# Second block of a two-block fp32 kernel: the order of a head pair's projections, a pair's end cut in two steps, and separate buffers

## The chip, the cores and the metric

One core of one Trainium2 chip runs the whole program. The metric is the device time of one execution in microseconds, the median over the runs shown.

## The reference

The program computes two blocks of two layers each over 512 tokens of width 1024, in fp32. The change touches the token mixing of the second block's layers, which has three kinds of heads of width 64:

```python
def layer(x, ...):                       # second block, cut
    a = dilated_mixture(q, k, v, bias_tab)            # 6 heads
    b = diff_attention(q1, q2, k1, k2, v, lam, bias_tab)   # 4 heads, then rms_norm per head
    c = causal_attention(q, k, v)                     # 6 heads, k and v from a 128-wide latent
...
def diff_attention(q1, q2, k1, k2, v, lam, bias_tab):
    a = probs(q1, k1) - lam * probs(q2, k2)           # two softmaxes per head
    return jnp.einsum('bhqk,bkhd->bqhd', a.astype(v.dtype), v)
```

Behind the mixing lie an output projection, a norm and a gated feed-forward network with 1024-wide weights.

## The kernel before

Every large product is computed three times: an operand is split into a high and a low part (`split`, lines 165 and 169), and `mm3` (lines 212, 213, 214) issues high by high, low by high and high by low. A matmul covers 128 rows of contraction by 512 tokens. TensorE also does all transposes (against `ident`), so ScalarE (ACT) and VectorE (DVE) spend their time on copies out of PSUM, splits of freshly loaded weights (`wh`, `wl`) and the softmax.

`second_mix` treats the heads in pairs, in the order of the list `UNITS`: differential 0, latent 0, differential 1, latent 1, dilated 0, latent 2, dilated 1, dilated 2. A pair has these parts.

- **Projection.** For a dilated or differential pair Q, K and V are each 24 matmuls `acc<-xt,wh` (`proj_t`), all into one of three PSUM buffers `acc`. A latent pair has 18 matmuls `acc<-ct,wh` in all, since its inputs are narrow.
- **V** (`vpair`, lines 991 to 1005): ACT copies the projection from PSUM to `vt` (line 996), TensorE transposes it in four pieces (line 999) into another `acc`, ACT takes the high part and DVE the low part (lines 1003, 1004).
- **Q and K of a differential pair** are split in four pieces of 32 rows, each an ACT instruction and behind it a DVE one on the same rows; GpSimd (POOL) makes a copy of each.
- **Attention** (`att2`): per head four score tiles of rising width (line 1025), a DVE instruction that adds the bias table and takes the maximum (line 1028), ACT's exp (line 1032), transposes of the weights (line 1058), a split, and the product with V (lines 1072 to 1075) whose two halves ACT and DVE put into `heads` (lines 1084, 1085). A differential head has two such softmaxes, combined on DVE (line 1048).
- **The pair's end** (`fin`): a factor per token and head, `inv`, is laid out along the rows by a DVE copy (line 1113, into `iv` or `sq`), transposed by TensorE (line 1118) and multiplied into the heads (lines 1120, 1122). A differential pair first takes the sum of squares (ACT line 1176, TensorE `half2` line 1179, DVE lines 1183 and 1184, POOL lines 219 and 222, DVE line 1186).

The order on each engine comes from a list scheduler that goes by priorities. The loop at the end of `second_mix` (lines 1306 to 1318) emits the projection of the next pair and then, at a priority raised by `AHEAD` (102), the two heads of this pair and the end of the pair before it:

```python
            if i + 1 < len(UNITS):
                nxt = proj(i + 1)
            with self.tc.high_priority(offset=AHEAD):
                for finish in att():
                    finish()
                if fin is not None:
                    fin()
            fin = fn
```

So the projection matmuls of the next pair fill TensorE while softmax runs on the other engines. During a turn whose next pair is a latent one there are 18 matmuls of 512 columns to fill with, otherwise 72; during the last turn there are none. `vt`, `iv`, `sq` and the latent pair's `qu` share one ring of two SBUF buffers (tag "vt").

Of the kernel before, what the change touches and what calls it, by code (L numbers as in the profile page):

```python
# [16 lines left out]
P = 128  # L17
# [100 lines left out]
class _Kernel:  # L118
# [107 lines left out]
    def setup(self):  # L226
# [20 lines left out]
        self.cF = self.small(4 * KT + P, "cF", 1)  # L247
# [707 lines left out]
    def second(self):  # L955
        tc, nc, A = self.tc, self.nc, self.A
        with ExitStack() as es:
# [4 lines left out]
            self.ropek = self.sp.tile([P, NX, 64], F32, name="ropek")  # L962
            nc.gpsimd.dma_start(self.ropek, A["ropek"])
# [125 lines left out]
    def second_mix(self, l, pool):  # L1089
# [8 lines left out]
        dl = pool.tile([P, 4, 32], F32, tag="dl", bufs=1, name="dl")  # L1098
        src = A["diff_lambda_2"][l]
        nc.gpsimd.dma_start(dl, bass.AP(tensor=src.tensor, offset=src.offset, ap=[[0, P], [32, 4], [1, 32]]))  # L1100
        pr = pool.tile([P, 2, 32], F32, tag="dlp", bufs=1, name="dlp")
        nc.vector.tensor_tensor(pr, dl[:, 0:4:2, :], dl[:, 1:4:2, :], op=ALU.mult)
        e2 = self.small(2, "lam2", 2)
        nc.vector.reduce_sum(e2, pr, axis=mybir.AxisListType.X)
        nc.scalar.activation(e2, e2, AF.Exp)
        nlam = self.small(1, "lam", 2)
        nc.vector.scalar_tensor_tensor(nlam, e2[:, 1:2], -li, e2[:, 0:1], op0=ALU.add, op1=ALU.subtract)
# [3 lines left out]
        def by_row(o, r8, sg, sq):  # L1111

            nc.vector.tensor_copy(
                sq.rearrange("p (a b) -> p a b", b=64), r8.unsqueeze(2).to_broadcast([P, 8, 64])
            )
            tp = self.tps()
            for t in range(NX):
                nc.tensor.transpose(tp[:, t * P : (t + 1) * P], sq[:, t * P : (t + 1) * P], self.ident)
# [4 lines left out]

        def dilated(p, o):
            Q, K, L = self.qk(pool), self.qk(pool), self.qk(pool)
            ps = self.proj_t(W, p * P)
# [9 lines left out]
            V = self.vpair(pool, self.proj_t(W, 768 + p * P))  # L1136
# [7 lines left out]
            def fin():  # L1144
                by_row(o, inv, None, pool.tile([P, SEQ], F32, tag="vt", bufs=2, name="iv"))

            return att, fin

        def differential(p, o):

            b0 = 1152 + p * P
# [39 lines left out]
        def latent(p, o):  # L1191
# [6 lines left out]
            for j in range(2):  # L1198
                kh, kl = Kb[j]
                self.split(kh[0:64], kl[0:64], pk[j * 64 : j * 64 + 64])  # L1200
# [307 lines left out]
```

## Time and profile before

| What | Value |
|---|---|
| median of 3 runs | 1983.33 us (1978.05 to 1986.85) |
| the profiled execution | 1981.64 us, its span 1979.9 us |
| mean granted TensorE clock | 0.993 of full speed |
| TensorE busy | 1901.3 us, 96% |
| TensorE weight loads (beside matmuls) | 1560.8 us, 79% |
| VectorE busy | 1203.6 us, 61% |
| ScalarE busy | 894.1 us, 45% |
| GpSimd busy | 169.7 us, 9% |

The span is the profiled execution of the program from its first to its last recorded instruction; the 1.7 us between it and the execution's own time lie around it. The mixing of the second block's two layers runs from about 731 to 914 us and from about 1370 to 1553 us. A row of the timeline is a start, a length, an engine, a line and the tiles; what stands in brackets is how long the engine had been idle and what released it. In a row of matmuls the lengths overlap, so the pace is read from start to start.

### The profile page before, as it was taken

How to read it: one execution, taken by the hardware profiler on the slowest of the kernel's cores; microseconds unless marked ns; L12 is line 12 of the kernel's file. 1: busy time of each engine (PE TensorE's matmuls, PEld its weight loads, DVE VectorE, ACT ScalarE, POOL GpSimd, SP SyncE). 2: the span in 40 equal slices, each digit the busy share in tenths (PEclk: the TensorE clock that was granted, in tenths of full speed). 3: DMA queues.
4: the chain of work that ended last, by engine and by line, in shares of the span. 5: the costliest groups of instructions: out<-in, count | busy, mean ns of one | idle time of the engine just before them, and what ended most of it. 6: DMA issues, size and time to landing. Idle time of an engine off the chain costs nothing.

```text
span 1979.9 us, 25710 instructions
## 1 busy us (share of the span) xinstructions
PE 1901.3 (96%) x9564; PEld 1560.8 (79%) x9564; DVE 1203.6 (61%) x2350; ACT 894.1 (45%) x1744; POOL 169.7 (9%) x299
## 2 busy tenths in 40 slices
PE   6999999999999999899999999999999999999997
PEld 3878788778878777777888888887777788888886
DVE  3759984375988578776733434366876664243444
ACT  4736662384755558665221322215866432132220
POOL 2100000030000132101200000012211010000001
PEclk9999999999999999999999999999999999999999
DMA  8414342042332361223432324325122332232421
GB/s 291 148 54 140 96 128 85 23 160 79 118 87 63 111 167 43 65 86 111 119 96 85 107 75 117 94 80 130 41 64 95 124 107 96 75 117 64 128 75 43
DMA packets 220448, 197.19 MB, mean 100 GB/s; under 512 B 30154, under 2 KB 178128, under 8 KB 220324
## 3 DMA queue, kind: packets, MB, share of 16 engines
q1 hardware_dynamic: 209940, 160.32, 27.3%
q0 software_dynamic: 10384, 35.24, 5.2%
q8 instruction: 75, 1.23, 0.3%
q14 instruction: 49, 0.40, 0.1%
HBM read 187.09 MB, written 12.03 MB: 101 GB/s over the span
## 4 chain that ended last, share of the span: by engine, by line
PE 80%; ACT 6%; DVE 5%; issue 2%; DMA 1%; POOL 1%; POOLq 0%; DVEq 0%; ACTq 0%; SPq 0%
PE acc L212 22%; PE acc L213 22%; PE acc L214 22%; PE sps L1025 2%; PE tps L792 1%; PE tps L1058 1%; ACT wh L165 1%; PE pv L803 1%; PE pv L1074 1%; PE pv L804 1%; DVE wl L169 1%; PE pv L1075 1%; PE tps L410 1%; DMA wr<-in_w_mod_dram 1%; ACT L L1032 1%
## 5 line engine op out<-in xcount | busy, mean ns | idle before, releaser
L165 ACT ACTIVATE wh<-wr 128x1024 fp32r<-128x1024 f32 (+3 forms) x299 | 311.9, 1045 | 605.3 <-PE acc L213 262.5
L169 DVE TENSOR_TENSOR wl<-wr,wh 128x1024 fp32r<-128x1024 f32 (+3 forms) x299 | 358.3, 1202 | 259.2 <-ACT wh L165 256.5
L212 PE MATMUL acc<-xt,wh 128*128 128x512 f32 (+1 forms) x1200 | 465.9, 388 | 2.1 <-DVE kb L169 1.7
L214 PE MATMUL acc<-xt,wl 128*128 128x512 f32 (+1 forms) x1200 | 464.7, 387 | 0.0
L213 PE MATMUL acc<-xt,wh 128*128 128x512 f32 (+1 forms) x1200 | 463.7, 386 | 0.0
L212 PEld LDWEIGHTS acc<-xt,wh 128*128 128x128 f32 x1200 | 226.2, 188 | 41.5 <-DVE kb L169 2.4
L214 PEld LDWEIGHTS acc<-xt,wl 128*128 128x128 f32 x1200 | 226.1, 188 | 39.8
L213 PEld LDWEIGHTS acc<-xt,wh 128*128 128x128 f32 x1200 | 226.2, 188 | 39.2
L212 PE MATMUL acc<-wh,ht 128*128 128x512 f32 (+1 forms) x494 | 193.1, 391 | 1.3 <-ACT ht L165 1.1
L213 PE MATMUL acc<-wl,ht 128*128 128x512 f32 (+1 forms) x494 | 192.1, 389 | 0.0
L214 PE MATMUL acc<-wh,ht 128*128 128x512 f32 (+1 forms) x494 | 191.7, 388 | 0.0
L165 ACT ACTIVATE pth<-tps 128x384 fp32r<-128x384 f32 (+1 forms) x176 | 90.1, 536 | 90.4 <-PE tps L792 48.4
L169 DVE TENSOR_TENSOR ptl<-tps,pth 128x384 fp32r<-128x384 f32 (+1 forms) x176 | 104.7, 614 | 25.4 <-ACT pth L165 24.1
L212 PEld LDWEIGHTS acc<-wh,ht 128*128 128x128 f32 x494 | 92.9, 188 | 23.0 <-ACT ht L165 2.6
L214 PEld LDWEIGHTS acc<-wh,ht 128*128 128x128 f32 x494 | 93.0, 188 | 21.2 <-DVE ht L169 0.4
L213 PEld LDWEIGHTS acc<-wl,ht 128*128 128x128 f32 x494 | 92.9, 188 | 20.0
L1032 ACT ACTIVATE L<-L,nm 128x512 f32<-128x512 f32 (+3 forms) x160 | 89.0, 557 | 31.2 <-DVE nm L1028 29.8
L1429 DVE SCALAR_TENSOR_TENSOR h<-h,acc 128x512 f32<-128x512 f32 (+1 forms) x50 | 33.2, 665 | 114.9 <-PE acc L214 114.9
L1395 DVE SCALAR_TENSOR_TENSOR th<-th,acc 128x512 f32<-128x512 f32 x42 | 28.9, 688 | 113.3 <-PE acc L214 113.1
L1028 DVE CUSTOM_DVE_ANT_0 L<-sps,T 128x512 f32<-128x512 f32 (+3 forms) x160 | 75.4, 487 | 25.4 <-PE sps L1025 23.5
L219 POOL TENSOR_SCALAR rv<-bna 128x1 f32<-128x1 f32 x16 | 18.8, 1173 | 789.0 <-DVE bna L1324 789.0
L214 PE MATMUL acc<-wh,xt 128*128 128x256 f32 (+2 forms) x256 | 85.1, 333 | 1.0 <-DVE xt L169 0.8
(317 smaller groups left out, 3352.2 us busy)
## 6 DMA issues: line engine op xcount, KB each, us to landing
wr<-in_w_in_dram SPq DMA_DIRECT2D x66, 512.0 KB, 4.6
wr<-in_w_gate_dram SPq DMA_DIRECT2D x44, 512.0 KB, 3.8
wr<-in_w_up_dram SPq DMA_DIRECT2D x44, 512.0 KB, 3.9
wr<-in_w_down_dram SPq DMA_DIRECT2D x42, 512.0 KB, 3.5
wr<-in_w_mod_dram SPq DMA_DIRECT2D x40, 512.0 KB, 4.5
wr<-in_w_o_dram SPq DMA_DIRECT2D x32, 256.0 KB, 3.6
T<-skew POOLq DMA_DIRECT2D x26, 256.0 KB, 2.9
x<-in_x_dram POOLq DMA_DIRECT2D x8, 512.0 KB, 7.1
```

Of the source, the lines that this page charges most:

```text
L165: self.nc.scalar.activation(out, in_, AF.Copy, scale=scale)
L169: self.nc.vector.tensor_tensor(out, in_, hi.bitcast(F32), op=ALU.subtract)
L212: mm(ps, lh, rh, start=(first and i == 0), stop=False)
L213: mm(ps, lh, rl, start=False, stop=False)
L214: mm(ps, ll, rh, start=False, stop=(last and i == n - 1))
L410: nc.tensor.transpose(v[:, k, :], src[:, (kb * 4 + k) * P : (kb * 4 + k + 1) * P], self.ident)
L792: nc.tensor.transpose(tp[:, hq * P : (hq + 1) * P], Ps[hq][:, i * P : (i + 1) * P], self.ident)
L1025: nc.tensor.matmul(ps[:, :w], x[:, tok], y[:, :w], start=(k == 0), stop=(k == len(s) - 1))
L1028: nc.vector.tensor_tensor_reduce(lc, ps[:, :n], T[:, SEQ - n : SEQ], 1.0, 3.0e38, op0=ALU.add, op1=ALU.min, accum_out=nm[:, i : i + 1],)
L1032: nc.scalar.activation(lc, lc, AF.Exp, bias=nm[:, i : i + 1], scale=-1.0, accum_out=sums[:, i : i + 1])
L1395: nc.vector.scalar_tensor_tensor(th, th, 0.5, pu, op0=ALU.mult, op1=ALU.mult)
L1429: nc.vector.scalar_tensor_tensor(h[:, c], h[:, c], ALPHA if gi == 0 else 1.0, ps, op0=ALU.mult, op1=ALU.add)
```

## The change

In `second_mix`, for all three kinds, V is projected first and copied to `vt` at once (`vcopy`); Q and K are projected behind it, and the transposes and the split of V come last. A pair's end becomes a list of two steps: laying out the factors (with the sum of squares ahead of it for a differential pair), and the transposes with the multiplication. One step is emitted behind each of the two heads of the next pair, where before the whole end came behind both. The laid-out factors have a buffer of their own (tag "iv", one buffer). Two small loads move: `ropek` is loaded per layer in place of once, and the differential pair's `lam` is computed inside the same short-lived pool as the latent inputs; `cF` of the conditioning goes to another pool.

```diff
+    def vcopy(self, pool, ps):
+        vt = pool.tile([P, SEQ], F32, tag="vt", bufs=2, name="vt")
+        self.nc.scalar.copy(vt, ps)
+        return vt
+
-    def vpair(self, pool, ps):
+    def vpair(self, pool, vt):
 
         nc = self.nc
-        vt = pool.tile([P, SEQ], F32, tag="vt", bufs=2, name="vt")
-        nc.scalar.copy(vt, ps)
...
-        def by_row(o, r8, sg, sq):
-
+        def spread(r8, iv=None):
+            iv = iv or pool.tile([P, SEQ], F32, tag="iv", bufs=1, name="iv")
             nc.vector.tensor_copy(
-                sq.rearrange("p (a b) -> p a b", b=64), r8.unsqueeze(2).to_broadcast([P, 8, 64])
+                iv.rearrange("p (a b) -> p a b", b=64), r8.unsqueeze(2).to_broadcast([P, 8, 64])
             )
+            return iv
+
+        def by_row(o, iv, sg=None):
+
             tp = self.tps()
...
+        def two_steps(o, inv):
+            ivs = []
+            return [lambda: ivs.append(spread(inv)), lambda: by_row(o, ivs[0])]
+
         def dilated(p, o):
             Q, K, L = self.qk(pool), self.qk(pool), self.qk(pool)
+            vt = self.vcopy(pool, self.proj_t(W, 768 + p * P))
             ps = self.proj_t(W, p * P)
...
-            V = self.vpair(pool, self.proj_t(W, 768 + p * P))
+            V = self.vpair(pool, vt)
...
         def differential(p, o):
 
             b0 = 1152 + p * P
+            vt = self.vcopy(pool, self.proj_t(W, b0 + 512))
...
-            V = self.vpair(pool, self.proj_t(W, b0 + 512))
+            V = self.vpair(pool, vt)
...
-            def fin():
-                sq = pool.tile([P, SEQ], F32, tag="vt", bufs=2, name="sq")
+            r8s = []
+
+            def sums():
+                sq = pool.tile([P, SEQ], F32, tag="iv", bufs=1, name="sq")
...
-                by_row(o, r8, sg, sq)
-
-            return att, fin
+                r8s.append(spread(r8, sq))
+
+            return att, [sums, lambda: by_row(o, r8s[0], sg)]
...
+            cp = es.enter_context(self.tc.tile_pool(name="c0", bufs=1, reuse_waits="tile"))
+            ropek = cp.tile([P, NX, 64], F32, tag="ropek", name="ropek")
+            nc.gpsimd.dma_start(ropek, A["ropek"])
+            nlam = lam(cp)
...
-        fin = None
+        fins = []
         for i in range(len(UNITS)):
             att, fn = nxt
             if i + 1 < len(UNITS):
@@ -1311,10 +1327,11 @@
             with self.tc.high_priority(offset=AHEAD):
                 for finish in att():
                     finish()
-                if fin is not None:
-                    fin()
-            fin = fn
-        fin()
+                    if fins:
+                        fins.pop(0)()
+            fins = fn
+        for f in fins:
+            f()
```

The number of matmuls stays at 9564. How the order moves is shown at three places on TensorE. In the changed kernel the lines of `second_mix` and `att2` are counted on by one or more (scores 1026, transposes of weights 1059, of V 1000, of factors 1127, sum of squares 1193).

**The second differential pair's turn, its first head.** Before, the score tiles `sps<-qk` stand between the 24 matmuls of the pair's own V projection, the end of which is:

```order
L1025 MATMUL sps_8046<-qk_7758,qk_7710 128x384
L214 MATMUL acc_7781<-xt_105,wl_7778 128x512
L1025 MATMUL sps_8047<-qk_7759,qk_7711 128x384
L212 MATMUL acc_7781<-xt_105,wh_7777 128x512
L213 MATMUL acc_7781<-xt_106,wh_7777 128x512
L1025 MATMUL sps_8054<-qk_7758,qk_7710 128x512
L214 MATMUL acc_7781<-xt_105,wl_7778 128x512
L1025 MATMUL sps_8055<-qk_7759,qk_7711 128x512
```

Here `acc_7781` collects V, and `qk_7710` and `qk_7711` are the pieces of the first head's K. In the changed kernel the last projection matmul of the pair (`acc_7766`, now K) stands ahead of the transposes of V and of every score of the pair; what is left to fill with are the latent pair's `acc<-ct`:

```order
L214 MATMUL acc_7766<-xt_105,wl_7763 128x512
L1059 MATMUL tps_7939<-ident_84,L_7901 128x128 x2
L1000 MATMUL acc_7808<-ident_84,vt_7710 128x128
L1059 MATMUL tps_7930<-ident_84,L_7901 128x128
L1059 MATMUL tps_7939<-ident_84,L_7901 128x128
L1000 MATMUL acc_7808<-ident_84,vt_7710 128x128 x3
L212 MATMUL acc_7973<-ct_7057,wh_7453 128x512
L213 MATMUL acc_7973<-ct_7058,wh_7453 128x512
L1075 MATMUL pv_7929<-pth_7935,V_7479 128x512
L1026 MATMUL sps_8030<-qk_7791,qk_7743 128x256
```

The scores moved from among the pair's own projection to behind it.

**The end of the second differential pair, as the first dilated pair starts.** Before, the sum of squares (`half2`) and the transposes of the factors (`ident,sq`) stand close together:

```order
L214 MATMUL acc_8478<-ct_7068,wl_7454 128x512
L1179 MATMUL tps_8458<-half2_7043,sq_8456 128x2 x4
L999 MATMUL acc_8484<-ident_84,vt_8482 128x128 x4
L212 MATMUL acc_8492<-ct_7068,wh_7453 128x512
L213 MATMUL acc_8492<-ct_7069,wh_7453 128x512
L1118 MATMUL tps_8472<-ident_84,sq_8456 128x128
L1058 MATMUL tps_8554<-ident_84,L_8529 128x128 x4
```

Between the two stand the transposes of one V and two matmuls of 512 columns. In the changed kernel the sum of squares stands half a turn earlier, among the dilated pair's projection matmuls:

```order
L213 MATMUL acc_8245<-xt_106,wh_8241 128x512
L214 MATMUL acc_8245<-xt_105,wl_8242 128x512
L212 MATMUL acc_8245<-xt_105,wh_8241 128x512
L1193 MATMUL tps_8392<-half2_7041,sq_8390 128x2
L213 MATMUL acc_8245<-xt_106,wh_8241 128x512
```

The transposes of its factors (`tps_8472`) follow 73 rows further down, past the dilated pair's last projection matmul and its first scores.

**The last turn, the third dilated pair.** Before, the transposes of the first head's weights `L` and of V stand right behind the last projection matmul:

```order
L214 MATMUL acc<-xt,wl 128x512
L1118 MATMUL tps<-ident,iv 128x128
L1058 MATMUL tps<-ident,L 128x128 x4
L1118 MATMUL tps<-ident,iv 128x128 x3
L999 MATMUL acc<-ident,vt 128x128 x4
L1058 MATMUL tps<-ident,L 128x128 x5
L1074 MATMUL pv<-pth,V 128x512
```

All 16 score matmuls of the pair stand further up, among the projection matmuls. In the changed kernel they stand behind the last of these, the first 8 of them ahead of any transpose of weights:

```order
L214 MATMUL acc<-xt,wl 128x512
L1127 MATMUL tps<-ident,iv 128x128 x4
L1000 MATMUL acc<-ident,vt 128x128 x4
L1026 MATMUL sps<-qk 128x256 x4
L1026 MATMUL sps<-qk 128x384 x2
L1026 MATMUL sps<-qk 128x512 x2
L1059 MATMUL tps<-ident,L 128x128 x3
```

The scores lost the projection matmuls that stood between them.

## Rows read from the trace of the kernel before

**Rows 1.** The page: busy time of the engines, and the chain that ended last.

```profile
PE 1901.3 (96%) x9564; PEld 1560.8 (79%) x9564; DVE 1203.6 (61%) x2350; ACT 894.1 (45%) x1744; POOL 169.7 (9%) x299
PE 80%; ACT 6%; DVE 5%; issue 2%; DMA 1%; POOL 1%; POOLq 0%; DVEq 0%; ACTq 0%; SPq 0%
```

**Rows 2.** Windows: stretch, length, busy time by engine, granted clock, DMA share, GB/s.

```profile
960.00:1300.00 340.00, 339.51 (x1579) 281.88 (x1578) 137.19 (x158) 89.12 (x110) 3.95 (x5) 1.00 0.33 100
731.00:746.00 15.00, 10.79 (x54) 7.33 (x52) 12.08 (x30) 12.48 (x28) 3.26 (x5) 1.00 0.25 72
770.00:796.00 26.00, 22.65 (x121) 17.11 (x120) 22.43 (x66) 21.53 (x60) 6.11 (x10) 1.00 0.15 41
819.00:846.00 27.00, 23.12 (x124) 18.65 (x124) 18.39 (x46) 19.01 (x44) 5.28 (x8) 0.94 0.24 69
902.00:914.00 12.00, 8.71 (x53) 6.21 (x52) 8.12 (x15) 7.11 (x15) 0.00 (x0) 1.00 0.20 66
sum 183.00, PE 166.60 PEld 130.44 DVE 142.63 ACT 129.61 POOL 27.40; mean PE 23.80 PEld 18.64 DVE 20.38 ACT 18.52 POOL 3.91
sum 183.00, PE 167.98 PEld 131.31 DVE 141.10 ACT 127.67 POOL 26.37; mean PE 24.00 PEld 18.76 DVE 20.16 ACT 18.24 POOL 3.77
```

**Rows 3.** Waits of TensorE, whole run: total us, times, longest.

```profile
PE acc L999 <- ACT vt L996: 8.3, 10, 1.4
PE tps L1118 <- DVE sq L1113: 4.8, 2, 2.4
```

**Rows 4.** Timeline of TensorE, 777 to 796 us, first layer.

```profile
777.42 0.40 PE L213 MATMUL acc<-xt,wh 128*128 128x512 f32 x1
777.65 0.39 PE L214 MATMUL acc<-xt,wl 128*128 128x512 f32 x1
...
795.97 0.50 PE L212 MATMUL acc<-xt,wh 128*128 128x512 f32 x1 [0.49 <-DVE kb L169]
```

**Rows 5.** Timeline of DVE, 776 to 784 us.

```profile
776.82 0.70 DVE L169 TENSOR_TENSOR qk<-acc,qk 32x512 fp32r<-32x512 f32 x1
...
778.17 0.69 DVE L1028 CUSTOM_DVE_ANT_0 L<-sps,T 128x512 f32<-128x512 f32 x1
...
778.78 0.69 DVE L169 TENSOR_TENSOR ptl<-tps,pth 128x512 fp32r<-128x512 f32 x1
...
781.57 1.93 DVE L1048 SCALAR_TENSOR_TENSOR L<-L,sum 128x128 f32<-128x128 f32 x4
```

**Rows 6.** Timeline of ACT and DVE, 729 to 731 us: pieces of a differential K.

```profile
729.00 0.59 ACT L165 ACTIVATE qk<-acc 32x512 fp32r<-32x512 f32 x1 [1.50 <-DVE qk L169]
730.34 0.59 ACT L165 ACTIVATE qk<-acc 32x512 fp32r<-32x512 f32 x1 [0.75 <-DVE qk L169]
```

**Rows 7.** Timeline of TensorE, 830 to 836 us, first layer.

```profile
830.27 0.66 PE L999 MATMUL acc<-ident,vt 128*128 128x128 f32 x4 [1.40 <-ACT vt L996]
830.68 0.48 PE L212 MATMUL acc<-ct,wh 128*128 128x512 f32 x1
...
835.99 0.33 PE L1118 MATMUL tps<-ident,sq 128*128 128x128 f32 x1 [2.40 <-DVE sq L1113]
```

**Rows 8.** POOL in the same stretch.

```profile
833.41 1.67 POOL L222 TENSOR_TENSOR rr<-rv,mhalf 128x8 f32<-128x8 f32 x1
```

**Rows 9.** Windows of 4 us: columns as in rows 2.

```profile
832.00:836.00 4.00, 1.60 (x12) 1.16 (x12) 1.79 (x6) 1.95 (x3) 2.68 (x4) 1.00 0.39 131
836.00:840.00 4.00, 4.00 (x17) 3.32 (x18) 2.47 (x4) 1.29 (x3) 0.40 (x1) 0.62 0.02 4
786.00:790.00 4.00, 2.40 (x10) 1.60 (x9) 2.54 (x11) 2.09 (x7) 1.86 (x2) 1.00 0.00 0
```

**Rows 10.** Timeline of TensorE and DVE, 905 to 914 us: the last turn.

```profile
905.48 1.00 PE L1058 MATMUL tps<-ident,L 128*128 128x128 f32 x5 [1.28 <-DVE ptl L169]
...
914.07 0.50 PE L212 MATMUL acc<-wh,ht 128*128 128x512 f32 x1 [0.56 <-ACT ht L165]
```

**Rows 11.** POOL ahead of the mixing, first layer.

```profile
703.88 0.25 POOL L1253 MEMSET xs<- 128x64 f32 x2 [4.02 <-DMA xs<-x]
```

More of the change, by code (lines that the diff above doesn't have):

```diff
@@ L246, in setup @@
         nc.vector.scalar_tensor_tensor(th, th, 1.0, c16, op0=ALU.add, op1=ALU.mult)
-        self.cF = self.small(4 * KT + P, "cF", 1)
+        self.cF = vp.tile([P, 4 * KT + P], F32, tag="cF", name="cF")
         nc.gpsimd.memset(self.cF, 0.0)
@@ L961, in second @@
             nc.gpsimd.dma_start(self.rope2, A["rope2"])
-            self.ropek = self.sp.tile([P, NX, 64], F32, name="ropek")
-            nc.gpsimd.dma_start(self.ropek, A["ropek"])
             self.half2 = self.sp.tile([P, 2], F32, name="half2")
@@ L1097, in second_mix, with lam @@
         li = 0.8 - 0.6 * math.exp(-0.3 * l)
[L1098 to L1107, printed above, removed]
+        def lam(pool):
+            dl = pool.tile([P, 4, 32], F32, tag="dl", bufs=1, name="dl")
+            src = A["diff_lambda_2"][l]
+            nc.gpsimd.dma_start(dl, bass.AP(tensor=src.tensor, offset=src.offset, ap=[[0, P], [32, 4], [1, 32]]))
+            pr = pool.tile([P, 2, 32], F32, tag="dlp", bufs=1, name="dlp")
+            nc.vector.tensor_tensor(pr, dl[:, 0:4:2, :], dl[:, 1:4:2, :], op=ALU.mult)
+            e2 = self.small(2, "lam2", 2)
+            nc.vector.reduce_sum(e2, pr, axis=mybir.AxisListType.X)
+            nc.scalar.activation(e2, e2, AF.Exp)
+            nlam = self.small(1, "lam", 2)
+            nc.vector.scalar_tensor_tensor(nlam, e2[:, 1:2], -li, e2[:, 0:1], op0=ALU.add, op1=ALU.subtract)
+            return nlam
         sg = self.small(1, "sg", 2)
         nc.vector.tensor_scalar(sg, self.col[:, 102 + l : 103 + l], 1.0 - li, None, ALU.mult)
-        def by_row(o, r8, sg, sq):
+        def spread(r8, iv=None):
+            iv = iv or pool.tile([P, SEQ], F32, tag="iv", bufs=1, name="iv")
             nc.vector.tensor_copy(
-                sq.rearrange("p (a b) -> p a b", b=64), r8.unsqueeze(2).to_broadcast([P, 8, 64])
+                iv.rearrange("p (a b) -> p a b", b=64), r8.unsqueeze(2).to_broadcast([P, 8, 64])
             )
+            return iv
+        def by_row(o, iv, sg=None):
             tp = self.tps()
             for t in range(NX):
-                nc.tensor.transpose(tp[:, t * P : (t + 1) * P], sq[:, t * P : (t + 1) * P], self.ident)
+                nc.tensor.transpose(tp[:, t * P : (t + 1) * P], iv[:, t * P : (t + 1) * P], self.ident)
             if sg is None:
@@ L1194, in latent @@
             self.mm3(pk, [(ukh[:, 1, hc], ukl[:, 1, hc], cT[2][0], cT[2][1])])
-            V = self.vpair(pool, pk)
+            vt = self.vcopy(pool, pk)
             pk = self.acc()
@@ L1200, in latent @@
                 self.split(kh[0:64], kl[0:64], pk[j * 64 : j * 64 + 64])
+            V = self.vpair(pool, vt)
             qs = []
@@ L1220, in att @@
                     yield self.att2(t2, [[(qh, kh), (qh, kl), (ql, kh)]], Tc, V, j, o, inv[:, j:8:2])
[L1222 to L1225 removed]
+            return att, two_steps(o, inv)
         def proj(i):
@@ L1240, in second_mix @@
         ws = self.wset(W, KT, 2, 1920, 416)
-        with self.tc.tile_pool(name="c0", bufs=1, reuse_waits="tile") as cp:
+        with ExitStack() as es:
+            cp = es.enter_context(self.tc.tile_pool(name="c0", bufs=1, reuse_waits="tile"))
+            ropek = cp.tile([P, NX, 64], F32, tag="ropek", name="ropek")
+            nc.gpsimd.dma_start(ropek, A["ropek"])
+            nlam = lam(cp)
             xss = []
@@ L1256, in second_mix @@
                 t1 = cp.tile([P, 2, 32], F32, tag="kt", bufs=2, name="kt")
-                rk = self.ropek[:, t, :]
+                rk = ropek[:, t, :]
                 nc.vector.tensor_tensor(t1[:, 0, :], ps[:, 384:416], rk[:, 0:32], op=ALU.mult)
```

7 lines of the change are left out of this document (1 added, 6 removed).

## The prediction

> **What bounds the kernel now.** I read the page's busy times first. TensorE is busy 96% of the span and makes 80% of the chain that ended last; DVE has 61%, ACT 45% [rows 1]. So a microsecond counts where TensorE stands still, and only there. The windows tell where that is [rows 2]. From 960 to 1300 us, in the feed-forward part, it idles 0.5 of 340 us. In the mixing it is busy 166.6 of 183 us in the first layer and 168.0 in the second: 16.4 and 15.0 us idle, 31.4 in all, 1.6% of the run. That is the most that the change can win by filling gaps, beside what the clock gives back. It adds no matmul; each unit of fill that it puts into one gap is taken from another.
>
> The list of waits names two gaps that the change aims at. TensorE's V transposes waited for ACT's copy `vt` ten times, 8.3 us in all; the transposes of the factors of a differential pair waited for DVE's `sq` twice, 2.4 us each [rows 3]. The timeline shows the second one: the first factor transpose starts at 835.99 after 2.40 us of waiting [rows 7], while POOL takes 1.67 us for eight columns of the reciprocal root [rows 8] with short DVE steps on both sides. [...]
>
> **The change part by part.** The sum is made against the profiled execution, 1981.64 us (span 1979.9 and 1.7 around it), which is 1.7 under the median of the runs. 0.5%, about what a measurement of this kernel can tell from no change, is 9.9 us.
>
> *V first, its transposes last.* The copy `vt` then has 48 matmuls of cover; at 0.23 us from start to start [rows 4] that is 11 us, so the wait L999 <- L996 goes. But what the V projection used to cover loses its cover. In the old order a pair's scores start while its own V is projected; now K comes last, and no score can start before K is projected and split. With three long projections ahead of it the pair loses up to 24 x 0.23 = 5.5 us of fill. Where the pair after it has 72 matmuls to give, that costs nothing, since they follow at once; this holds for pairs with a dilated or differential one behind them. It hurts where a pair's scores stand ahead of a latent pair's 18 matmuls: the first differential pair at the start (d), the second one (a), the first dilated pair (b); and in the last turn, which has none (c).
>
> (a) *Second differential pair* (770 to 796 us; before, TensorE idle 26.00 - 22.65 = 3.4 us with DVE busy 22.4 of 26 [rows 2]). By the new order, DVE's work from the first low piece of K to the instruction that frees an `acc` for new fill is: four pieces of K at 0.70; two heads' weight splits, 0.69 for 512 columns and less for the narrower two, 1.6 per head; four softmaxes of four tiles, of which the widest takes 0.69, some 1.64 to 1.96 each; the combination 1.93; two V, two `kb`, one `qu`, two `heads`, a factor copy and a multiplication of 512 columns, 0.4 to 0.7 each, 5.6 together; 1 us of small ones [rows 5]. That is 20 to 22.7 us. TensorE has in the same stretch 18 matmuls at 0.23 (4.1), 16 score tiles (2.6, scaled by columns), the products with V of two heads (2.3), and 25 transposes, four of which take 0.41 from start to start [rows 7]: 2.5; with the refill after small pieces, 12 to 13.5. Idle is then 6.5 to 10.7, that is 3.1 to 7.3 more. I take +5, the middle.
>
> The K pieces bear on this. In the trace ACT's next piece waits for DVE's last, 1.34 us from one to the next, though each lies in other rows [rows 6]; four in series are 5.4 us. [...]
>
> (b) *First dilated pair* (819 to 846 us; idle 27.00 - 23.12 = 3.9 [rows 2], with the clock 5.4). Here both waits lay: V's 1.40 and the factors' 2.40 [rows 7]. The *two-step end* takes the sum of squares half a turn forward, among projection matmuls, so the POOL step of 1.67 has that long and the 2.40 goes. By the same count DVE has 14.8 to 15.4 us in the new stretch and TensorE 12 to 13.5: idle 1.3 to 3.4. Gain between 2.0 and 4.1; I take -3.
>
> (c) *The last turn* (902 to 914 us; 8.7 busy, idle 3.3, of which 1.28 wait for a weight split and 0.56 for the last `ht` [rows 2, 10]). The 16 score tiles, 2.6 us of TensorE, now fall here, with a softmax chain ahead of the first transpose. If the chain lengthens by just these, idle stays: 0. If all the fill that stood among them (16 matmuls, 3.7 us) turns into waiting, +3.7. V no longer gates the first product, which speaks for the low end; I take +0.5.
>
> (d) *Start of the mixing* (731 to 746 us, idle 4.2 [rows 2]). Its V waits go, but DVE, busy 12.1 of the 15 us, brings the first scores no earlier, because K's pieces now come after the last projection matmul. 0, between -2 (the waits won) and +1.
>
> (e) *The laid-out factors' own buffer* takes a DVE or ACT instruction's wait for `vt` away; those copies are 0.4 us and covered by fill: 0. *`ropek` and `lam`* put two POOL DMAs per layer ahead of the reciprocal root of the latent inputs. In the first layer POOL waited there for a transfer of `xs` until 703.88 anyway [rows 11]; 0, to +1 if the load is late. `cF`: the memory only, 0.
>
> (f) *The clock.* The stall of (b) is gone; but the stretch of (a) is some 60% busy. The window with 2.40 of 4 us busy did not lower the clock afterwards, that with 1.60 did [rows 9]. +0.5, between 0 and +3.
>
> Per layer: 5 - 3 + 0.5 + 0 + 0 + 0.5 = +3; two layers +6: 1981.6 + 6 = **1988 us** (rounded).
>
> **The rivals.** *Faster:* the waits come back whole. V's 8.3 and the factors' 4.8 [rows 3] with two times 1.5 of clock are 16; if (a) and (c) are hidden because the scheduler's order lets the latent fill last, 1981.6 - 16 = 1966 us. For it: that these waits end nowhere else in the list. Against: DVE's 22.4 of 26 us in (a), which needs the 24 matmuls beside it.
>
> *Slower:* DVE becomes the bound of (a), with the clock falling there. Idle at its upper end is +7.3, a clock fall like that of 836 us 1.5, the tail 2.5, with the gain in (b) 2: +9.3 per layer, 2000 us. It decides once more than about 5.5 us of idle is added in (a). For it: nothing but 18 matmuls stands between the last K matmul and the next projection. [...]
>
> *The change does not do what it says:* the steps are only emitted earlier, and the scheduler's order leaves the same waits in sum, moved: 0, 1982 us. The order shows the factor transposes apart from their sum of squares, so this is unlikely as a whole; it falls within no change.
>
> **How the numbers follow.** The forecast and the case of no effect, whose ends lie within 9.9 us of the profiled run: 0.49. Faster 0.22, slower 0.29, as (a) has more known cost than the waits have certain gain. The range goes to both rivals' times less a bit on the fast side and more on the slow one, where the terms (c) and (f) can add: 1969 to 2006. Left out are a tenth on each side.
>
> **What would show it.** Right: no row for V transposes waiting on `vt`, none of 2.4 us for `sq`; TensorE busy in the window of the second differential pair falls by 4 to 6 us against the length, and the releaser of its gaps is DVE (`kb`, `V` or `nm`); the granted clock stays 1.00 around the first dilated pair; the matmul count is 9564. Wrong: (a) idles no more than 4 us, or the last turn is over 3 us longer in idle, or a new wait on POOL ahead of the mixing.

## The result and the profile after

The changed kernel takes 2010.14 us (median of four runs, 2004.67 to 2010.71) against 1983.51: the ratio is 1.0129, interval 1.0112 to 1.0147. It is slower by 26.6 us; 1988 was forecast, with 2006 as the upper end.

The page of the changed kernel, span and busy times, against [rows 1]:

```profile
span 2008.7 us, 25702 instructions
PE 1918.3 (96%) x9564; PEld 1570.4 (78%) x9564; DVE 1206.0 (60%) x2350; ACT 893.1 (44%) x1744; POOL 167.9 (8%) x300
```

The work is the same: as many matmuls, DVE and ACT instructions, and DVE and ACT within 3 us of their busy times. TensorE is busy 17 us longer on the same matmuls, which is the first sign of the clock (its mean granted clock is 0.986, against 0.993 before), and idle some 12 us longer. The list of its waits, to be read against [rows 3]:

```profile
PE sps L1026 <- DVE nm L1029: 13.5, 22, 2.3
PE sps L1026 <- DVE qk L169: 8.1, 6, 2.4
...
PE tps L1127 <- DVE iv L1118: 4.1, 2, 2.1
PE acc L1000 <- DVE V L1005: 3.5, 2, 1.8
PE sps L1026 <- POOL qk L1149: 2.9, 6, 0.6
```

The two waits that the change aimed at are gone: V's transposes no longer wait for `vt`, nor the factors of the differential pairs for 2.4 us. In their place the scores wait, for K's split (`qk`, 8.1 us) and for the softmax that frees their PSUM buffer (`nm`, 13.5).

For the rest of this text each layer's mixing is cut at the same five places of TensorE's order in every kernel: the first transpose of the latent inputs, the first dilated or differential projection matmul behind each of the three latent pairs' 18 matmuls, and the first output projection matmul. I call the four stretches start, second differential, first dilated and rest; the middle two hold the turn ahead of that pair and its own scores. The windows of these stretches, first layer; the sum is over both layers' eight. Kernel before:

```profile
731.35:746.27 14.92, 10.44 (x52) 7.11 (x50) 12.00 (x32) 12.72 (x30) 3.01 (x5) 1.00 0.25 72
746.27:795.97 49.70, 46.23 (x246) 35.94 (x246) 44.78 (x127) 40.49 (x107) 10.44 (x16) 1.00 0.16 43
795.97:846.48 50.51, 45.90 (x245) 36.87 (x246) 37.98 (x90) 33.81 (x78) 7.50 (x12) 0.97 0.23 63
846.48:914.07 67.59, 63.68 (x339) 50.32 (x337) 47.59 (x108) 42.63 (x102) 6.11 (x10) 1.00 0.28 90
...
sum 367.87, PE 335.27 PEld 262.33 DVE 284.85 ACT 259.42 POOL 54.07; mean PE 41.91 PEld 32.79 DVE 35.61 ACT 32.43 POOL 6.76
```

Changed kernel:

```profile
732.63:752.93 20.30, 14.64 (x53) 9.96 (x51) 16.58 (x42) 15.35 (x37) 5.63 (x9) 0.78 0.22 66
752.93:810.95 58.02, 50.34 (x245) 38.34 (x244) 45.65 (x123) 40.30 (x104) 10.08 (x16) 0.91 0.12 32
810.95:857.40 46.45, 44.23 (x235) 34.65 (x234) 33.50 (x82) 30.68 (x72) 6.93 (x10) 0.99 0.24 69
857.40:929.20 71.80, 66.02 (x348) 52.03 (x346) 50.95 (x113) 44.97 (x106) 9.16 (x16) 0.99 0.33 109
...
sum 392.64, PE 349.39 PEld 269.34 DVE 293.33 ACT 262.62 POOL 63.59; mean PE 43.67 PEld 33.67 DVE 36.67 ACT 32.83 POOL 7.95
```

Start +5.4, second differential +8.3, first dilated -4.1, rest +4.2; in the second layer +3.7, +8.0, -4.4, +3.6. Of the 28.8 us that the span grew, 24.8 lie here, 1.3 ahead of the first mixing, 2.0 between the two and 0.7 behind. The 24.8 split by these windows: idle (length less TensorE's busy time) goes from 32.6 to 43.3, +10.7. What the lower clock cost, each stretch's busy time times one less its granted clock, goes from 5.3 to 15.8 over the eight, +10.5; this is an estimate. The other 3.6 stays unexplained.

The cut ahead of the rest moved a little: ten matmuls that stood in the first dilated stretch before (TensorE's 245 against 235) now stand in the rest (339 against 348). At the 0.11 to 0.23 us from start to start of such matmuls in the trace they are some 1.4 us, an estimate. Without them these two stretches are -2.7 and +2.8 in the first layer, -3.0 and +2.2 in the second.

**Where it starts.** TensorE in the changed kernel, first layer; the first row is the pair's last projection matmul:

```profile
731.96 0.39 PE L214 MATMUL acc<-xt,wl 128*128 128x512 f32 x1
732.19 0.60 PE L1000 MATMUL acc<-ident,vt 128*128 128x128 f32 x4
732.63 1.04 PE L1288 MATMUL tps<-ident,xs 128*128 128x128 f32 x8
736.06 0.35 PE L1026 MATMUL sps<-qk 96*128 96x256 f32 x1 [2.40 <-DVE qk L169]
...
741.55 0.63 PE L214 MATMUL acc<-ct,wl 128*128 128x512 f32 x1
741.98 0.63 PE L213 MATMUL acc<-ct,wh 128*128 128x512 f32 x1
```

V's transposes come without a wait, and then the first score waits for K, 4.1 us behind the last projection matmul. DVE in the same stretch, the low pieces of K and the first softmax tile:

```profile
735.23 0.68 DVE L169 TENSOR_TENSOR qk<-acc,qk 32x512 fp32r<-32x512 f32 x1
...
737.33 0.69 DVE L169 TENSOR_TENSOR qk<-acc,qk 32x512 fp32r<-32x512 f32 x1
...
740.01 0.69 DVE L169 TENSOR_TENSOR qk<-acc,qk 32x512 fp32r<-32x512 f32 x1
...
743.45 0.70 DVE L169 TENSOR_TENSOR qk<-acc,qk 32x512 fp32r<-32x512 f32 x1 [1.19 <-ACT qk L165]
...
744.90 0.29 DVE L1029 CUSTOM_DVE_ANT_0 L<-sps,T 128x128 f32<-128x128 f32 x1
```

The same in the kernel before: TensorE's first score and the last projection matmul, then DVE's first and last low piece of K and the first softmax tile:

```profile
729.11 0.36 PE L1025 MATMUL sps<-qk 96*128 96x256 f32 x1
...
731.12 0.39 PE L214 MATMUL acc<-xt,wl 128*128 128x512 f32 x1
```

```profile
728.29 0.68 DVE L169 TENSOR_TENSOR qk<-acc,qk 32x512 fp32r<-32x512 f32 x1
...
733.67 0.70 DVE L169 TENSOR_TENSOR qk<-acc,qk 32x512 fp32r<-32x512 f32 x1
...
740.15 0.29 DVE L1028 CUSTOM_DVE_ANT_0 L<-sps,T 128x128 f32<-128x128 f32 x1
```

There the first score stood 2.0 us ahead of the last projection matmul. Three of K's four pieces were done under V's 24 matmuls, and the last one 3.0 us into the stretch. Now the four pieces share DVE and ACT with the latent pairs' `ct` and `kb`, are spread over 8.9 us, and the first softmax tile comes 4.75 us later on the clock of the run, 3.5 later after the stretch's own shift of 1.28. And the wait is paid twice, once as idle time and once at the clock behind it. Windows of 4 us of the changed kernel:

```profile
732.00:736.00 4.00, 1.66 (x14) 1.33 (x12) 3.08 (x5) 3.79 (x6) 2.04 (x3) 1.00 0.12 30
736.00:740.00 4.00, 2.47 (x8) 1.76 (x9) 3.48 (x5) 1.93 (x4) 1.20 (x3) 0.65 0.43 121
740.00:744.00 4.00, 3.97 (x14) 2.74 (x12) 1.94 (x3) 2.33 (x4) 2.15 (x4) 0.50 0.41 131
...
928.00:932.00 4.00, 3.01 (x9) 2.13 (x10) 2.73 (x6) 1.86 (x6) 0.00 (x0) 0.54 0.94 327
932.00:936.00 4.00, 4.00 (x13) 3.15 (x12) 3.36 (x9) 1.60 (x5) 0.00 (x0) 0.61 0.02 6
```

In the window at a granted clock of 0.50 matmuls of 512 columns start 0.43 us apart (741.55 to 741.98), not 0.23 as from 744.53 to 744.76. The last two windows lie at the end of the mixing, behind this wait, TensorE and then DVE (the second layer has the same wait of 2.06 us, until 1580.72, and no fall behind it: 1.00 from 1580 to 1588 us):

```profile
928.46 1.08 PE L1127 MATMUL tps<-ident,iv 128*128 128x128 f32 x4 [2.06 <-DVE iv L1118]
```

```profile
927.16 0.70 DVE L1086 TENSOR_TENSOR heads<-pv,heads 64x512 f32<-64x512 f32 x1
927.89 0.43 DVE L1118 COPY iv<-inv 128x512 f32<-128x512 f32 x1
```

The last pair's factors are laid out only behind the last use of `heads`, because the one buffer `iv` still holds those of the pair before. Before, they lay in a ring of two, and the copy stood clear of the end; TensorE transposed the factors of both pairs without a wait:

```profile
907.09 0.42 DVE L1113 COPY iv<-inv 128x512 f32<-128x512 f32 x1
...
912.58 0.93 PE L1118 MATMUL tps<-ident,iv 128*128 128x128 f32 x7
```

### The profile page after: what moved, and what is told of

Same layout as the page of the kernel before. It is cut to its first block, busy times and chain, and to the rows that moved or that the text cites. A ratio compares the mean times of both kernels' runs of the same rounds, so it can differ in the third digit from the quotient of the medians.

```text
span 2008.7 us, 25702 instructions
## 1 busy us (share of the span) xinstructions
PE 1918.3 (96%) x9564; PEld 1570.4 (78%) x9564; DVE 1206.0 (60%) x2350; ACT 893.1 (44%) x1744; POOL 167.9 (8%) x300
## 4 chain that ended last, share of the span: by engine, by line
PE 80%; DVE 6%; ACT 5%; issue 2%; POOL 1%; DMA 1%; DVEq 0%; POOLq 0%; ACTq 0%; SPq 0%
PE acc L212 22%; PE acc L214 22%; PE acc L213 22%; PE tps L1059 2%; PE sps L1026 2%; PE tps L792 2%; PE pv L803 1%; ACT wh L165 1%; PE pv L1075 1%; PE pv L804 1%; DVE wl L169 1%; PE pv L1076 1%; DVE L L1029 1%; PE tps L410 1%; POOL rr L222 1%
## 5 line engine op out<-in xcount | busy, mean ns | idle before, releaser
L1033 ACT ACTIVATE L<-L,nm 128x384 f32<-128x384 f32 (+3 forms) x160 | 88.9, 557 | 33.5 <-DVE nm L1029 32.2
L214 PE MATMUL acc<-wh,xt 128*128 128x256 f32 (+2 forms) x256 | 84.9, 332 | 1.0 <-DVE xt L169 0.8
L212 PE MATMUL acc<-wh,xt 128*128 128x256 f32 (+2 forms) x256 | 84.5, 331 | 0.1
```

The costliest lines, as they stand in the source:

```text
L212: mm(ps, lh, rh, start=(first and i == 0), stop=False)
L214: mm(ps, ll, rh, start=False, stop=(last and i == n - 1))
L1033: nc.scalar.activation(lc, lc, AF.Exp, bias=nm[:, i : i + 1], scale=-1.0, accum_out=sums[:, i : i + 1])
```

## The experiments

The change has three parts that can be undone apart: V first, the two steps, and the buffers (with the loads moved to make room). My theory after the two traces was the order: K comes last, nothing covers its split, and the clock falls in the gaps. Its rivals were the two-step end and the loads moved onto POOL's queue. All 17 kernels, each beside runs of the kernel before on the same chip (its medians were 1982.9 to 1984.7, so a difference between two kernels of different groups of runs carries up to 1.8 us of that):

| Kernel | Median, us | Ratio to before |
|---|---|---|
| end undone | 2010.89 | 1.0134 (1.0115 to 1.0154) |
| V last | 1993.78 | 1.0047 (1.0029 to 1.0065) |
| buffers only | 1989.67 | 1.0033 (1.0022 to 1.0045) |
| V first where covered | 1990.67 | 1.0036 (1.0023 to 1.0049) |
| loads only | 1983.14 | 0.9995 (0.9985 to 1.0004) |
| two steps for one pair, own buffer | 1979.00 | 0.9973 (0.9962 to 0.9984) |
| V transposes five times | 2011.04 | 1.0130 (1.0114 to 1.0145) |
| scores twice | 2011.75 | 1.0129 (1.0110 to 1.0147) |
| change, shared ring | 2003.48 | 1.0098 (1.0078 to 1.0118) |
| one pair, last factors in the ring | 1971.95 | 0.9942 (0.9920 to 0.9963) |
| Q, V, K | 2002.91 | 1.0099 (1.0080 to 1.0118) |
| no combination | 2006.16 | 1.0120 (1.0096 to 1.0145) |
| V last in differential pairs | 1993.99 | 1.0051 (1.0032 to 1.0069) |
| best, V first where covered | 1977.95 | 0.9967 (0.9957 to 0.9977) |
| no low part of K | 2004.16 | 1.0100 (1.0079 to 1.0121) |
| V last, no low part of K | 1988.69 | 1.0022 (1.0009 to 1.0035) |
| two steps for one pair, shared ring | 1983.12 | 0.9988 (0.9976 to 1.0001) |

**The parts undone.** The first, the end in one piece:

```diff
                 for finish in att():
                     finish()
-                    if fins:
-                        fins.pop(0)()
+                for f in fins:
+                    f()
```

> The changed kernel with the pair's end in one piece again, behind both heads of the next pair; V first stays. Order theory (K comes last and nothing covers its split; the clock falls in these gaps): the loss of 27 us stays or grows, 2008 to 2018 us, since the end that was split won about 4 us per layer at the first dilated pair. End theory (the two steps and their single buffer cost the time): back to 1980 to 1990. Loads theory (ropek and lam on POOL's queue): unchanged at 2010.

2010.89: the time stays while V is first, as the order theory said and the loads theory too; the two steps by themselves don't carry the loss. The trace tells something more. With the end in one piece, too, the list has no wait on `sq`; at its place TensorE waits for V's low part:

```profile
848.83 0.51 PE L212 MATMUL acc<-ct,wh 128*128 128x512 f32 x1 [2.04 <-DVE V L1005]
```

So in the changed kernel it is not shown that the two steps took the 2.40 away; with V last it is (below). Then V last (the same edit in all three kinds), and both undone:

```diff
-            vt = self.vcopy(pool, self.proj_t(W, b0 + 512))
...
-            V = self.vpair(pool, vt)
+            V = self.vpair(pool, self.vcopy(pool, self.proj_t(W, b0 + 512)))
```

> The changed kernel with V projected last again in all three kinds; the end in two steps, its buffer and the moved loads stay. Order theory: 1974 to 1984 us, the stall of 2.4 us and its clock fall gone, the V waits back. End theory: 2000 or more, still some 20 us above the kernel before. Loads theory: 2005 to 2010.

> Both undone: V last, the end in one piece; only the own buffer of the laid-out factors and the moved loads stay. Order theory and end theory: 1981 to 1987 us, within 4 us of the kernel before. Loads theory: 2000 or more.

1993.78 and 1989.67. V first carries the larger part, but neither kernel is back at 1984: the order theory's expectations missed, by 10 and 3 us. In the trace of the second, TensorE shows the late factors of the last pair again:

```profile
917.16 0.63 PE L1127 MATMUL tps<-ident,iv 128*128 128x128 f32 x4 [2.05 <-DVE iv L1118]
```

To part the own buffer from the loads, its tag was set back to `vt`, here and for `sq`, with the rest as in the run before:

```diff
-            iv = iv or pool.tile([P, SEQ], F32, tag="iv", bufs=1, name="iv")
+            iv = iv or pool.tile([P, SEQ], F32, tag="vt", bufs=2, name="iv")
...
```

> As the run with both undone, and the laid-out factors share the buffers of vt again as in the kernel before: only the loads of ropek and lam and the place of cF differ from it. If the loads cost the 6 us: 1987 to 1993. If the own buffer does, by the order it gives: 1981 to 1986.

1983.14: the loads cost nothing, the single buffer 6.5 us (1989.67 less 1983.14; 7.2 when each is set against the kernel before beside it). This kernel also prices a clock fall: its two layers run the first dilated stretch with the same order and the same idle time, 4.6 us, once with a fall and once without.

```profile
800.99:852.45 51.46, 46.85 (x244) 37.81 (x245) 38.00 (x90) 33.84 (x78) 7.52 (x12) 0.93 0.22 62
...
1439.83:1488.87 49.04, 44.41 (x245) 35.74 (x245) 37.84 (x90) 33.75 (x78) 7.49 (x12) 1.00 0.23 65
```

It costs 2.4 us, and whether it comes is not fixed by the order alone. The spread of one kernel's runs goes with the clock, too: of the changed kernel's four, the fastest (2004.67) has a mean granted clock of 0.989, the slowest (2010.71) of 0.986, and 0.003 of 1918 us of TensorE's time is some 5.8 us, against a spread of 6.0.

**Which pairs.** V last in the two differential pairs alone:

> The changed kernel with V last in the two differential pairs alone. Theory that the open split of the differential K carries the loss: the start returns to 15 to 17.5 us and the second pair's stretch to 53 us, 1994 to 2001 us. If the dilated pairs carry it: 2006 to 2011.

1993.99, with a start of 17.2 us and a second differential stretch of 52.0; the first softmax tile is back at 8.8 us into the start, as before. This is the time of V last everywhere (1993.78): 16.1 us of V first's loss are the differential pairs', whose Q and K take four pieces each to split, every piece an ACT and a DVE instruction. The other kinds cost nothing net. V first kept where 72 matmuls follow, without and with the better order found below:

> The changed kernel with V last again in the two differential pairs and in the first and third dilated pair, whose scores stand ahead of a latent pair's 18 matmuls or of none; V first stays in the three latent pairs and the second dilated one. Order theory, if it is the missing fill that decides: 1972 to 1984 us, as with V last everywhere or a little less. If V first costs by itself, wherever it stands: 1990 to 2000.

> The fastest order so far (1971.95) with V first in the latent pairs and the second dilated one, where 72 matmuls of the pair behind follow. If V first wins there what the V waits cost: 1967 to 1971. If those waits are filled anyway: 1970 to 1975.

1990.67 and 1977.95 (against 1993.78 and 1971.95). The first lies in the range of "V first costs by itself", but that range had taken V last to be at 1984 or below. V first won 3 us on the one order and lost 6 on the other (4.6 against the kernel before beside each), so by itself it is not worth having there; neither expectation of the second held.

**Is K's split the open work?** V between Q and K in the dilated and differential pairs, so that V is early and K still last:

```diff
+                if scale is None:
+                    vt = self.vcopy(pool, self.proj_t(W, b0 + 512))
                 ps = self.proj_t(W, c)
...
```

> The changed kernel with V projected between Q and K in the dilated and differential pairs: V still early, K still last. Theory that the split of K lies open behind the last projection matmul: 2003 to 2012 us as with V first. If it is V's place at the head of the pair (its buffer held over 48 matmuls) that costs: 1990 to 1998, nearer to V last.

2002.91, at the edge of the first expectation, with a start of 19.9 and 19.0 us and a second differential stretch of 56.4 and 56.2: K last keeps 9.1 of the 16.4 us that V first costs over V last, and V's place one more projection ahead is worth the other 7.2. Then the DVE half of K's split left out, with V first and with V last:

```diff
-                    self.split(t[r], t[low], ps[r], scale)
+                    if scale:
+                        self.split(t[r], t[low], ps[r], scale)
+                    else:
+                        nc.gpsimd.memset(t[low].bitcast(F32), 0.0)
+                        nc.scalar.copy(t[r], ps[r])
```

> The changed kernel with the low part of the differential K left out (set to zero by POOL ahead of time, ACT alone copies the four pieces): the series of four ACT and four DVE pieces, 5.4 us, becomes four ACT pieces, 2.4 us. Theory of the open split: TensorE gets its first scores 2 to 3 us sooner at the start and at the second differential pair, 1996 to 2004 us. If the split is covered: 2008 to 2012.

> The same part left out with V last (two steps, own buffer), whose median was 1993.8. Theory of the open split: V's own matmuls covered it there, 1989 to 1994 us, less than half of what it gives with V first. If DVE's work as such decides: the same 6 to 12 us less as with V first, 1982 to 1988.

2004.16 and 1988.69: 6.0 and 5.1 us less, much the same with V first as with V last (the first is 0.2 above its range, the second between its two). The theory of the open split had asked for less than half with V last, so the DVE half by itself is not what lies open. Which member is open this run can't tell, for its edit adds work for POOL, whose fills stand ahead of the copies that the scores need. POOL and then TensorE's first score, with V first:

```profile
733.82 0.52 POOL L1177 MEMSET qk<- 32x512 f32 x1
734.40 3.27 POOL L1179 CAST qk<-qk 32x512 fp32r<-32x512 f32 x5
```

```profile
735.72 0.39 PE L1026 MATMUL sps<-qk 96*128 96x256 f32 x1 [2.76 <-POOL qk L1179]
```

Freed from DVE, the score waits as long for POOL, which four added fills of some 0.5 us each help to keep busy. The first softmax tile comes 11.6 us into the start, against 12.3 in the changed kernel and 8.8 before: most of its delay is left. That the chain projection, ACT piece, DVE piece, copy, score is open as a whole fits the runs, but no run shortened all of it. One more member stands in no theory above, the first head's bias table `T`. Its load is issued on POOL's queue, behind K's copies. The kernel before, and the changed one:

```profile
736.49 1.17 POOL L950 DMA_DIRECT2D T<-skew  x2 [2.38 <-DVE V L1004]
```

```profile
740.56 1.18 POOL L950 DMA_DIRECT2D T<-skew  x2
```

These loads landed some 3 us (2.8 to 3.2) behind their issue, in the changed kernel 1.4 us ahead of the first softmax tile (744.90). So the load came later along with K's copies, and may hold the first tile back by itself; no run moves it alone.

The combination of the two softmaxes left out, to see how far DVE sets the pace:

```diff
-            for i in range(NX):
-                c = slice(off[i], off[i] + (i + 1) * P)
-                nc.vector.scalar_tensor_tensor(
-                    L[:, c], L2[:, c], r2[:, i : i + 1], L[:, c], op0=ALU.mult, op1=ALU.add
-                )
```

> The changed kernel without the four DVE instructions per differential head that subtract the second softmax from the first (1.93 us each head, eight heads in the run, 15.4 us of DVE in all); this part of the result is left out. If DVE sets the pace of the unfilled stretches: 1996 to 2005 us, the stretch of the second differential pair 2 to 4 us shorter in each layer. If latency or TensorE does: 2007 to 2012.

2006.16, between the two expectations: of 15.4 us of DVE taken away, 4 came back. Start and second differential stretch together went from 78.3 to 75.5 us in the first layer, with TensorE then waiting 7.8 us in the run for ACT's exp. So DVE alone doesn't set the pace in these stretches: in the start it is busy 16.6 us, ACT 15.4 and TensorE 14.6.

**Can the clock be held up?** Transposes of V of the differential pairs issued five times, and their scores issued twice:

```diff
-        for t in range(NX):
+        for t in list(range(NX)) * again:
...
-            for ps, s in zip(pss, subs):
+            for ps, s in [a for a in zip(pss, subs) for _ in subs]:
```

> The changed kernel with the four transposes of V of each differential pair issued five times into the same place: 64 matmuls of 128 columns more in the run, no result changed. They stand just ahead of the first scores, where TensorE waits 2.40 us for the split of K. Clock theory (half of the added time is the lower clock that follows such a wait): the granted clock stays at 1.00 around 736 us and 1388 us, and the run gets faster by 4 to 8 us although it does more, 2002 to 2007. If only the waits cost: 2010 to 2013, the clock unchanged or the gain nil.

> The changed kernel with each score matmul of the differential pairs issued twice: 64 matmuls of 256 to 512 columns more in the run, some 10 us of TensorE by themselves. Clock theory: those in unfilled stretches take the place of waiting and keep the clock up, 2002 to 2010. If TensorE's own work decides: 2015 to 2020.

2011.04 and 2011.75. The expectation of the clock theory missed in both: neither got faster. The first met its other expectation (only the waits cost), the second lies between its two. TensorE's added matmuls took the place of waiting. Over the eight stretches its idle time (43.3 us in the changed kernel) is 35.4 and 35.1:

```profile
sum 391.07, PE 355.71 PEld 275.50 DVE 292.61 ACT 260.07 POOL 64.68; mean PE 44.46 PEld 34.44 DVE 36.58 ACT 32.51 POOL 8.09
sum 391.35, PE 356.23 PEld 280.92 DVE 292.05 ACT 262.50 POOL 63.55; mean PE 44.53 PEld 35.12 DVE 36.51 ACT 32.81 POOL 7.94
```

In the first the 16 extra transposes took the place of the long wait, and the granted clock held until past 744 us (0.95 from 742 to 746); then it fell all the same:

```profile
730.73 2.34 PE L1000 MATMUL acc<-ident,vt 128*128 128x128 f32 x20
```

```profile
746.00:750.00 4.00, 3.79 (x10) 2.71 (x10) 3.81 (x15) 2.83 (x9) 0.54 (x1) 0.50 0.24 68
```

From 730 to 746 us no single wait was over 0.94 us there, and in the 4 us behind it the granted clock was 0.50. So here a fall did not need one long wait, and filling one gap moved it. The run also parts the delay of the first softmax tile: in the first layer, with the clock up (matmuls of 512 columns 0.23 us apart until 742 us), it came 11.2 us behind the last projection matmul, against 12.9 in the changed kernel and 9.0 before. By this difference, an estimate, some 1.7 of the 3.9 us of delay is the lower clock, and the rest the order. That the clock's 10.5 us would vanish with the idle time is argued, not shown.

**The buffer and the two steps.** The whole change with the shared ring (tags as above):

> The changed kernel with the laid-out factors in the ring of vt again (two buffers shared), V first and two steps kept. In its trace the last pair's factors are copied only after the pair before has used the single buffer, and their transposes wait 2.06 us right ahead of the output projection, where the granted clock then falls. Buffer theory: that wait goes, with its clock fall, 2 to 5 us per layer: 2000 to 2006. If the wait is due to the last turn's chain and not to the buffer: 2008 to 2012.

2003.48: 6.7 us less, as the buffer theory had it; the wait on `iv` (4.1 us in the changed kernel) is gone from the list of TensorE's waits. The two steps for the second differential pair alone, V last:

```diff
                 for finish in att():
                     finish()
+                    if fins and UNITS[i - 1][:2] == ("B", 1):
+                        fins.pop(0)()
+                for f in fins:
+                    f()
```

> V last and the moved loads and own buffer as in the run with both undone, but the end in two steps for the second differential pair alone. If the two steps pay where a POOL step stands in the chain and cost elsewhere: the stretch of the first dilated pair shrinks from 48 or 50 us to 43, the stretch before and the one behind stay, 1976 to 1983 us. If the gain there is always given back behind it: 1987 to 1992.

1979.00, faster than before; the first dilated stretch is 43.7 us in both layers. Of what is left, the last pair's late factors were next; they go into the ring, where V is done:

```diff
+            if last:
+                iv = pool.tile([P, SEQ], F32, tag="vt", bufs=2, name="iv")
             iv = iv or pool.tile([P, SEQ], F32, tag="iv", bufs=1, name="iv")
...
```

> V last, two steps for the second differential pair alone, own buffer, and the last pair's factors in the ring of vt. Buffer theory: the 2.06 us wait and the clock fall behind it go in both layers, 1969 to 1975 us against 1979.0 with the single buffer. Otherwise 1977 to 1981.

1971.95, 0.9942 of the kernel before, the fastest kernel found: 11.0 us under the median beside it (1982.92). Its windows of the first dilated stretch and the rest, first layer:

```profile
800.49:844.16 43.67, 42.27 (x233) 34.24 (x234) 35.99 (x85) 30.91 (x73) 6.97 (x12) 1.00 0.31 85
844.16:913.71 69.55, 65.46 (x348) 51.73 (x346) 49.01 (x112) 45.50 (x107) 6.04 (x11) 1.00 0.26 80
```

43.67 us against 50.51, with the clock at 1.00. Eleven matmuls, some 1.6 us by the same estimate, stand in the rest here (69.55 against 67.59); both stretches together are 4.9 us shorter. Whether this needs the own buffer, with the ring shared by all:

> V last, moved loads, the ring of vt shared as before, the end in two steps for the second differential pair alone. If splitting that one chain is the whole gain: the first dilated pair's stretch 43 to 45 us, the rest as before, 1970 to 1976 us, as with the own buffer and the last pair in the ring (1971.95). If the gain needs the own buffer: 1979 to 1985.

1983.12: no gain that can be measured. The first dilated stretch is 48.2 us, the `sq` wait replaced by one of 1.87 for a weight split and V's 1.52 still there. The gain took both: the chain cut in two, and its factors in a buffer that doesn't compete with `vt`. (That buffer for all but the last pair, with the end in one piece, was not run.)

## Why the prediction was wrong

The direction of the likeliest case was right and its size was not: +3 us per layer was forecast, +13.9 and +10.9 came. Term by term:

- **(d) the start: the step that failed most.** "0, between -2 (the waits won) and +1", because "DVE, busy 12.1 of the 15 us, brings the first scores no earlier". The premise looked at one side: with K last the first scores don't only fail to come earlier, they come later. The first one went from 2.0 us ahead of the last projection matmul to 4.1 behind it, and the first softmax tile came 3.5 us later in the stretch. Measured +5.4 and +3.7, some 3 of it clock in the first layer by the estimate above (14.64 us busy at 0.78). That V's place in the differential pairs does it is shown (17.2 and 8.8 us again with V last there); by which member of the chain, K's pieces, their copies or the load of `T`, stays open.
- **(a) the second differential pair: right in its idle time.** +5 of 3.1 to 7.3; idle rose from 3.5 to 7.7 us (58.02 less 50.34), +4.2, as costed, and +4.6 in the second layer. The stretch grew by 8.3 and 8.0, because the clock, 0.91 and 0.94 there, took most of the rest by the same estimate (4.5 and 3.0 us). That belongs to (f). (DVE's items as listed add up to 21.1 to 22.4 us, not 20 to 22.7, which hardly moves the middle; the refill in TensorE's 12 to 13.5 stands in no row.)
- **(b) the first dilated pair: right in size, its cause only in part.** -3 of -4.1 to -2.0; the stretch shrank by 4.1 and 4.4, some 2.7 and 3.0 without the matmuls that left it, and the clock there is 0.99. The two steps were to do it; with V first and the end in one piece the wait on `sq` was gone as well, and another stood in its place.
- **(c) the last turn: mis-sized.** +0.5, upper end +3.7; the rest grew by 4.2 and 3.6, some 2.8 and 2.2 without the matmuls that came to it. With the ring shared the rest is 70.56 and 70.54 us, 1.2 and 0.9 less: so the buffer, which was not costed here, is the smaller part. The larger is not shown to be the scores, which were costed: with V last in all pairs (two steps, own buffer), where they have their projection matmuls back, the rest is 72.3 and 72.7 us. Its cause stays open.
- **(e) the own buffer: the second failed step.** It was put at 0, as taking a wait away. One buffer in place of a ring of two adds one where two pairs' ends meet, at the end of the mixing: 2.06 us in each layer and in places a clock fall behind it (0.54 and 0.61 in the first layer of the changed kernel, 1.00 in the second), 6.5 us in the run. *`ropek` and `lam`* at 0: right (1983.14).
- **(f) the clock: the third.** +0.5 of 0 to +3 per layer; measured some 10.5 over both, spread over (a) and (d), so it is not to be added to them. The forecast took the window that had 2.40 of 4 us busy without a fall [rows 9] as safe ground. In the changed kernel the clock fell to 0.60 in the 4 us behind this window:

```profile
804.00:808.00 4.00, 2.50 (x13) 1.82 (x13) 3.58 (x11) 3.47 (x11) 0.00 (x0) 1.00 0.01 2
```

The 1.5 us of clock in (b)'s 5.4 and in both rivals' sums is an estimate from one window of [rows 9], 4 us at one less the 0.62 granted; no run shows it by itself. What the runs show of such a fall is 2.4 us, between the two layers of the loads-only kernel (51.46 and 49.04).

The slower rival came nearest. It had the clock falling in (a), and named 2000; it was given 0.29. But its bound was DVE, and 15.4 us of DVE taken away gave back 4; its condition, over 5.5 us of idle added in (a), was not met (4.2 and 4.6); and it had nothing for the start. Undoing part by part, the 27 us add up as loads 0, own buffer +6.5, two steps +4.1 with V last, V first +0.2 outside the differential pairs and +16.1 in them. The parts are not independent: with V first, two steps or one makes no difference (2010.14 and 2010.89).

The faster rival had the waits come back whole. Both did go from the list, and TensorE waited at the scores instead.

The signs of being right came true almost to the last (no wait on `vt`, none of 2.4 us on `sq`, DVE as the releaser in (a)), while the time was wrong. None of them looked at the start or at the clock in (a).

## What to carry to other kernels

When a projection is moved ahead, ask what it was covering: here, as fits the runs, the four-piece split of the differential K, now last, with all that hangs on it (16.1 us in those pairs). Cut a chain only where a slow step stands in it (here two steps for the one pair took 10.7 us off, 1989.67 to 1979.00, and for all pairs they added 4.1), and give the cut piece a buffer that neither competes with its neighbours (1983.12 us with the shared ring) nor is single where two users meet (1979.00 us with the last pair's factors in the single buffer, 1971.95 with them in the ring). Cost a thinly filled stretch twice, once as idle time and once at the lower clock, for here the second, an estimate, was as large as the first (10.5 and 10.7 us).

## What was not expected of the hardware

The granted clock fell in a stretch without a wait over 0.94 us, and with one order and one idle time it fell in one layer and not in the other (51.46 against 49.04 us), so one profile of a kernel doesn't tell whether a given fall belongs to it. In the changed kernel the pace came back behind a busy stretch: TensorE was busy 3.97 of the 4 us from 740 at a granted clock of 0.50, and from 744.53 matmuls of 512 columns started 0.23 us apart again. Added matmuls put a fall off here, from the window at 736 us (0.65) to that at 746 (0.50), and won no time (2011.04 and 2011.75 us, against 2010.14).
